# Values of each pair of token blocks projected beside the pair's sums, products on raw weights first, output-weight steps paced

## The chip, the cores and the metric

One core of a Trainium2 chip runs the whole layer. The metric is the device time of one execution in microseconds (us). The engines: TensorE (PE; its weight loads are the row PEld), VectorE (DVE), ScalarE (ACT), GpSimd (POOL) and SyncE (SP), which issues DMAs here and computes nothing. ACT issues DMAs too.

## What is computed

One mixer layer over 2048 latent tokens (a 32 x 64 grid) and 256 context tokens, width 1024: normalisation and modulation give h; one projection of h into eight groups of 512 columns; neighbourhood attention on one half of the groups, retention on the other; gates; one output projection with its own gate; a residual and a last normalisation.

```python
p = h @ w_in      # h: (2304, 1024), w_in: (1024, 4096)
# columns: NA q 0 | NA k 512 | NA v 1024 | NA gate 1536 | RET q 2048 | RET k 2560 | RET v 3072 | RET gate 3584
y = concat(neighbourhood_attention(q, k, v, k_ctx, v_ctx) * silu(gate), retention(rq, rk, rv) * silu(rgate))
out = rmsnorm(x + ada_gate * (y @ w_out))
```

Everything is float32. Each operand is split into a high part, rounded to fp32r, and a low part, the rest; a product is three matmuls: high x high, low x high, high x low.

## The kernel before

The latent tokens are four blocks of 512, the context is block 4. The parts of h of a block are two tiles of SBUF, high and low, of 2 MB each. Blocks 0 and 1 lie in the pool `hx`, 2 and 3 in `hy`, and there is no room for more: from some point on, blocks lie in DRAM (`hS`) and are reloaded. Weights of 256 columns come as two raw tiles `st` (four in all, so two sets of columns) and are split into `whi` and `wlo` by `w_split` (ACT casts, POOL or DVE subtracts); there are two pairs.

The program is one list of instructions per engine, in the order in which the Python code emits them, and a DMA stands on its issuing engine's queue in that order. A `unit` is one projection of 256 columns: `u_k` (K), `u_v` (values of attention, 256 tokens), `u_rk`, `u_rv`, `u_rq` (retention). One is 48 matmuls of 256 columns for values, in eight yields. `tick()` issues the stores deferred by earlier units, and `hooks` are functions called between pieces.

The order of the work around the change:

- K windows (`window(b)`, L485, b = 0 to 4): 32 steps each, in which the blocks' h is also prepared; window 4 is the context's and half as long.
- Values of blocks 2 and 3, 8 units, two spill steps (a DMA of 0.5 MB into `hS`) after each, so 16 in all; then 2 units of context values; then 8 units of blocks 0 and 1, beside which `h_sums(T, 0, 1)` (L514) makes four sums of half blocks in the tiles of `hy`. It is ten functions: VectorE and POOL add and subtract, ACT rounds the high part (L524), DVE or POOL make the low part (L525).
- `strassen(T, 0, 1, ...)`: six sets of 256 columns (`SETS`: NA gate, RET gate, NA q). A set (`w_set`, L609) computes a 2 x 2 block product for the two token blocks by seven products of half size instead of eight. Four products use a sum of weights, made by `w_sums` (L569) in four parts p0 to p3 from the raw weights; POOL makes the low parts (L580), ACT the high (L579). Parts of the next set's sums are called at four steps in the set: p0 after the second product, then p1, p2 and p3. Blocks 0 and 1 are spilled meanwhile, one DMA a step.
- Reload of blocks 2 and 3 into `hx`, and four units of the context for retention (`u_rk`, `u_rv`). Then 4 units `u_rv` of 256 columns at 3072 for blocks 2 and 3, beside `h_sums(T, 2, 3)`.
- `strassen(T, 2, 3, ...)`, with `wo_steps`: `wo_open`, eight `wo_gate` (each adds a row block of w_ada into the gate row `gacc`, L688), `wo_row` (two matmuls that spread the row, L695), eight `wo_mul` m0 to m7 (a row block of w_out times the gate row, L699, split and stored). The row block is one tile, `wraw`, loaded by SP (L685) after each step. One step of the list is called per step of a set.
- 24 fill steps (`LEAD`): a fill step is one yield of the units of a stream of retention projections; attention calls the rest of the stream between the parts of its 128 tiles, and the retention comes behind. `NF` counts 44 units of 8 steps.

Line numbers are those of the kernel before. In `w_set` the products are issued in this order, with `W` the weights' sums, `t` the tokens' sums and `b` raw blocks:

```python
nc.scalar.copy(yb, prod(W["a11"], b11))
V(xa, prod(W["a12"], b21), yb, ALU.add)
step(0)
m4 = prod(W["a22"], t4)
...
V(xb, prod(W["s2"], t2), yb, ALU.add)
step(1)
m5 = prod(W["s1"], t1)
V(yb, prod(W["s3"], t3), xb, ALU.add)
...
step(2)
m3 = prod(W["s4"], b22)
...
step(3)
```

Of the kernel before, what the change touches and what calls it, by code (L numbers as in the profile page):

```python
# [82 lines left out]
def hybrid_kernel(ctx: ExitStack, tc: tile.TileContext, a: dict, out: bass.AP):  # L83
# [390 lines left out]
    fseq = [(u_rv, 3328), (u_rk, 2560), (u_rq, 2048), (u_rk, 2816), (u_rq, 2304)]  # L474
    fseq += [(u_rv, 3328), (u_rv, 3072), (u_rk, 2560), (u_rq, 2048)]
    MID = [(2560, u_rk), (2816, u_rk), (3328, u_rv), (3072, u_rv)]
    wseq = [1280, *SETS, *[c0 for c0, _ in MID], *SETS, fseq[0][1], fseq[1][1]]
    wcur = []

    def load_w():  # L480
        if wseq:
# [1065 lines left out]
```

## Time and profile before

| | us |
|---|---|
| median of 3 runs | 1485.26 (1485.07 to 1489.99) |
| the profiled execution | 1483.65 |
| its span in the trace | 1481.8 |
| TensorE busy in the span | 1335.8 (90%) |
| VectorE, ScalarE, POOL busy | 787.6, 590.4, 628.7 |
| mean granted clock of TensorE | 0.962 of full |

The span is what the trace covers; the time of the execution has about 2 us around it. A row of the timeline is: start in us, duration of the stretch in us, engine, line of the kernel, operation, output tile <- input tiles, shape, count in the stretch, and in brackets how long the engine had been idle and what released it.

### The profile page before, as it was taken

The page shows a single profiled execution, that of the slowest core. Times are in us where ns is not written, and L with a number is a line of the kernel's source. Part 1 is how long each engine was busy: PE and PEld are TensorE (multiplying, and loading weights), DVE is VectorE, ACT ScalarE, POOL GpSimd, SP SyncE. Part 2 cuts the span into 40 slices and gives each one's busy share as a digit, 9 for nine tenths or more (in the row PEclk, how much of TensorE's full clock was granted, in tenths as well). Part 3 has the DMA queues.
Part 4 walks back from the last instruction along what each step waited for, and adds up shares of the span by engine and source line. Part 5 has one row for each costly group of instructions (what it writes and reads, how often), then busy time and mean ns, then how long its engine had stood idle before and what let it go on. Part 6 is the DMA issues. An engine that isn't in the chain of part 4 may idle for free.

```text
span 1481.8 us, 23106 instructions
## 1 busy us (share of the span) xinstructions
PE 1335.8 (90%) x8236; PEld 1165.8 (79%) x8236; DVE 787.6 (53%) x1420; ACT 590.4 (40%) x1245; POOL 628.7 (42%) x585
## 2 busy tenths in 40 slices
PE   6989999489989397766999999999999989999997
PEld 2467999478878285546998999999999879888886
DVE  5786116333424463342678777777665554444435
ACT  4544212233231233322655655555665233334332
POOL 4442312354444454542454643445453234544442
PEclk9999999699999598888999999999999999999999
DMA  9544692366483056656886779995754998655533
GB/s 307 163 157 142 226 303 94 116 221 229 163 310 130 29 171 199 221 205 191 202 230 198 210 221 266 265 250 163 209 159 127 293 283 260 227 174 168 170 122 121
DMA packets 228596, 292.49 MB, mean 197 GB/s; under 512 B 17537, under 2 KB 169217, under 8 KB 227458
## 3 DMA queue, kind: packets, MB, share of 16 engines
q1 hardware_dynamic: 192674, 227.30, 51.4%
q10 hardware_dynamic: 35808, 63.72, 12.2%
q8 instruction: 66, 1.08, 0.3%
q14 instruction: 48, 0.39, 0.1%
HBM read 193.43 MB, written 97.52 MB: 196 GB/s over the span
## 4 chain that ended last, share of the span: by engine, by line
PE 42%; issue 4%; DVE 4%; DMA 4%; POOL 3%; ACT 2%; SPq 1%; ACTq 0%; POOLq 0%; DVEq 0%
PE mm L1391 10%; PE mm L365 8%; PE sS L952 5%; PE mm L354 4%; PE tr L979 3%; PE po L1000 3%; PE mm L1114 2%; PE tr L981 2%; PE po L1002 2%; DMA v<-rvS 1%; PE mm L1303 1%; PE mm L1302 1%; PE mm L1301 1%; POOL g L704 1%; PE mm L1282 1%
## 5 line engine op out<-in xcount | busy, mean ns | idle before, releaser
L365 PE MATMUL mm<-whi,hhi 128*128 128x256 f32 x768 | 225.4, 293 | 7.8 <-DVE o L406 7.8
L365 PE MATMUL mm<-wlo,hhi 128*128 128x256 f32 x768 | 218.6, 285 | 3.6 <-POOL wlo L338 3.6
L365 PE MATMUL mm<-whi,hlo 128*128 128x256 f32 x768 | 217.8, 284 | 0.0
L983 ACT CAST pt<-tr 128x640 fp32r<-128x640 f32 (+1 forms) x128 | 95.7, 748 | 153.9 <-PE tr L981 152.5
L365 PEld LDWEIGHTS mm<-whi,hhi 128*128 128x128 f32 x768 | 147.5, 192 | 8.0 <-issue 8.0
L972 POOL TENSOR_SCALAR sp<-sp,stt 128x640 f32<-128x640 f32 (+2 forms) x128 | 103.5, 812 | 116.8 <-DVE stt L971 100.2
L365 PEld LDWEIGHTS mm<-wlo,hhi 128*128 128x128 f32 x768 | 146.9, 191 | 4.5 <-POOL wlo L338 4.5
L365 PEld LDWEIGHTS mm<-whi,hlo 128*128 128x128 f32 x768 | 147.8, 192 | 0.0
L989 DVE TENSOR_TENSOR pt<-tr,pt 128x640 fp32r<-128x640 f32 (+1 forms) x128 | 113.9, 890 | 63.6 <-ACT pt L983 62.3
L961 DVE CUSTOM_DVE_ANT_0 sp<-sS,nb 128x640 f32<-128x640 f32 (+2 forms) x128 | 105.4, 824 | 31.1 <-DMA nb<-in_rpb_t_dram 24.0
L966 ACT ACTIVATE sp<-sp,stt 128x640 f32<-128x640 f32 (+2 forms) x128 | 107.4, 839 | 29.8 <-DVE stt L961 28.7
L622 PE MATMUL mm<-hhi,whi 128*128 128x512 f32 x336 | 101.4, 407 | 17.9 <-ACT whi L579 15.1
L338 POOL TENSOR_TENSOR wlo<-st,whi 128x256 fp32r<-128x256 f32 (+1 forms) x75 | 86.2, 1165 | 68.3 <-ACT whi L336 62.4
L952 PE MATMUL sS<-k,q 128*128 128x256 f32 (+3 forms) x512 | 100.4, 318 | 14.0 <-DMA q<-qS 10.6
L354 PE MATMUL mm<-hhi,whi 128*128 128x512 f32 x256 | 107.3, 419 | 0.0
L354 PE MATMUL mm<-hlo,whi 128*128 128x512 f32 x256 | 101.0, 394 | 5.5 <-DVE hlo L271 2.3
L354 PE MATMUL mm<-hhi,wlo 128*128 128x512 f32 x256 | 101.2, 395 | 0.0
L952 PEld LDWEIGHTS sS<-k,q 128*128 128x128 f32 x512 | 82.7, 189 | 21.0 <-issue 10.7
L1391 PE MATMUL mm<-wor,y 128*128 128x512 f32 x384 | 95.4, 397 | 1.2 <-DVE xt L1400 1.2
L580 POOL TENSOR_TENSOR whi<-st,whi 128x512 fp32r<-128x512 f32 x48 | 63.3, 1340 | 76.6 <-ACT whi L579 75.1
L622 PEld LDWEIGHTS mm<-hhi,whi 128*128 128x128 f32 x336 | 65.7, 196 | 35.0 <-ACT whi L579 15.7
L622 PE MATMUL mm<-hhi,wlo 128*128 128x512 f32 x240 | 73.9, 424 | 18.3 <-ACT o L651 10.7
(252 smaller groups left out, 3059.8 us busy)
## 6 DMA issues: line engine op xcount, KB each, us to landing
st<-in_w_in_dram SPq DMA_DIRECT2D x58, 512.0 KB
q<-qS SPq DMA_DIRECT2D x64, 256.0 KB
k<-kS SPq DMA_DIRECT2D x16, 576.0 KB
kS<-o SPq DMA_DIRECT2D x16, 512.0 KB
hS<-hhi SPq DMA_DIRECT2D x16, 512.0 KB
hS<-hlo SPq DMA_DIRECT2D x16, 512.0 KB
qS<-o ACTq DMA_DIRECT2D x16, 512.0 KB
hhi<-hS SPq DMA_DIRECT2D x16, 512.0 KB
```

The source lines that it names most:

```text
L338: eng.tensor_tensor(l, r, f(h), ALU.subtract)
L354: nc.tensor.matmul(pm[:, :n], ww[:, k, cs], h[:, k, :], start=(k == 0 and i == 0), stop=(k == KC - 1 and i == 2))
L365: nc.tensor.matmul(pm[:, t * WG:(t + 1) * WG], h[:, k, o:o + P], ww[:, k, :], start=(k == 0 and i == 0), stop=(k == KC - 1 and i == 2))
L580: nc.gpsimd.tensor_tensor(t[:, 1], r, f(t)[:, 0], ALU.subtract)
L622: nc.tensor.matmul(pm, ww[:, k, :], hh[:, k, :], start=(k == 0 and i == 0), stop=(k == KH - 1 and i == 2))
L952: nc.tensor.matmul(o, hd["q"][i][:, hl, j * P:(j + 1) * P], k, start=(hl == 0), stop=(hl == 1))
L961: nc.vector.tensor_tensor_reduce(T["sp"][:, :n], T["s"], nbz[big][:, o:o + n], -1.0, 3e38, ALU.add, ALU.min, T["st"][:, 0:1])
L966: nc.scalar.activation(sp[:, :n], sp[:, :n], AF.Exp, bias=st[:, 0:1], scale=-1.0, accum_out=st[:, 1:2])
L972: nc.gpsimd.tensor_scalar(sp[:, :n], sp[:, :n], st[:, 2:3], 0.0, ALU.mult, ALU.add)
L983: nc.scalar.copy(pt[:, :ng_ + 2, 0, :], tr[:, :ng_ + 2, :])
L989: nc.vector.tensor_tensor(pt[:, :n, 1, :], tr[:, :n, :], f(pt)[:, :n, 0, :], ALU.subtract)
L1391: nc.tensor.matmul(pm, yy[:, k, :], ww[:, k, sl], start=(k == 0 and i == 0), stop=(k == 3 and i == 2))
```

## The change

1. The spill of blocks 2 and 3 moves from the value units into the K windows 3 and 4: one DMA at every fourth step.
2. The values of blocks 2 and 3 are no longer projected ahead of the first sets. They are projected after the reload, beside `h_sums(T, 2, 3)`, as those of blocks 0 and 1 are beside `h_sums(T, 0, 1)`. A new function `values` does both. The weights at 1024 and 1280 are loaded and split a second time for that. Every fifth yield calls one of the ten functions of the sums, the first sum of the weights (p0) is made after the fifth unit, the others after the loop.
3. The four units `u_rv` at 3072 that stood there go into the attention fill; `NF` is 48 units, `LEAD` 32 steps. Blocks 3 and 2 change places in the order of the fill and of the reload.
4. In a set the order of products is a11, a12, s4, a22, s2, s3, s1. Of the weights' sums p1 and p2 are called together at the third step, and p3 holds two cuts and the next load. The split of the weights that follow the last set moves to the third step too.
5. In `h_sums`, `fourth` is all on VectorE, in a tile used in halves, and the low part of key 4 goes to POOL.
6. In `wo_steps` a step without work stands after g1, g3, g5 and g7, and another ahead of the row.

```diff
-LEAD = 24
+LEAD = 32
...
-    fseq = [(u_rv, 3328), (u_rk, 2560), (u_rq, 2048), (u_rk, 2816), (u_rq, 2304)]
+    fseq = [(u_rv, 3072), (u_rk, 2560), (u_rq, 2048), (u_rv, 3328), (u_rk, 2816), (u_rq, 2304)]
...
-    wseq = [1280, *SETS, *[c0 for c0, _ in MID], *SETS, fseq[0][1], fseq[1][1]]
+    wseq = [1280, *SETS, 2560, 2816, 3328, 3072, 1024, 1280, *SETS, fseq[0][1], fseq[1][1]]
...
             run_acts(32 * b + n)
+            if b > 2 and n % 4 == 3:
+                spill_step()
...
-            (G if key < 3 else V)(t[:, 1, ks, :], d, f(t)[:, 0, ks, :], ALU.subtract)
+            (V if key == 3 else G)(t[:, 1, ks, :], d, f(t)[:, 0, ks, :], ALU.subtract)
...
-            o = env["st"].tile([P, 2, 512], F32, name="o3", bufs=1)
-            d, e = o[:, 0, :], o[:, 1, :]
+                tl["o"] = env["st"].tile([P, 2, 512], F32, name="o3", bufs=1)
+            d = tl["o"][:, k % 2, :]
             V(d, bh[:, k, :], ah[:, k, :], ALU.subtract)
-            G(e, bl[:, k, :], al[:, k, :], ALU.subtract)
-            V(d, d, e, ALU.add)
+            V(d, d, bl[:, k, :], ALU.add)
+            V(d, d, al[:, k, :], ALU.subtract)
...
         def p2():
+            cut("s4", 3, 0, a12)
+
+        def p3():
+            cut("s3", 2, 1, a21)
             cut("s1", 2, 0, a22)
-            cut("s3", 2, 1, a21)
-
-        def p3():
-            cut("s4", 3, 0, a12)
             load_w()
 
-        return W, [p0, p1, p2, p3]
+        return W, [p0, None, lambda: (p1(), p2()), p3]
...
-        return [None, p1, None, load_w]
+        return [None, None, p1, None]
...
         step(0)
+        m3 = prod(W["s4"], b22)
+        fin(oa, 0, A)
         m4 = prod(W["a22"], t4)
-        fin(oa, 0, A)
+        step(1)
         V(xb, prod(W["s2"], t2), yb, ALU.add)
-        step(1)
-        m5 = prod(W["s1"], t1)
         V(yb, prod(W["s3"], t3), xb, ALU.add)
         oc, (_, xc) = out_tile()
         V(xc, m4, yb, ALU.add)
+        V(xb, m3, xb, ALU.add)
+        fin(oc, 1, A)
+        step(2)
+        m5 = prod(W["s1"], t1)
         od, (_, xd) = out_tile()
...
+    def values(ws, bb, hs, W):
+        ahead = [None] * 4
+        vu = [(w, c0, tp) for w, c0 in zip(ws, (1024, 1280)) for b in bb for tp in (2 * b, 2 * b + 1)]
+        y = 0
+        for n, (w, c0, tp) in enumerate(vu):
+            for _ in u_v(w, c0, tp):
+                y += 1
+                if hs and y % 5 == 0:
+                    hs.pop(0)()
+            tick()
+            if n == 4:
+                W, ahead = w_sums(wcur.pop(0))
+                ahead[0]()
+        while hs:
+            hs.pop(0)()
+        ahead[2]()
+        ahead[3]()
+        return W
...
-    wo_steps = [wo_open, None] + [g(k) for k in range(8)] + [wo_row] + [m(k) for k in range(8)]
+    seq = [wo_open] + [g(k) for k in range(8)] + [None, wo_row] + [m(k) for k in range(8)]
+    wo_steps = []
+    for n, e in enumerate(seq):
+        wo_steps += [e, None] if n in (2, 4, 6, 8) else [e]
```

Three places, as the engines' instruction lists have them. SP's queue at the end of the K windows, before (`kS` are the stores of K, `st` weights, `vB` values, `hS_0_91` and `hS_1_92` block 2's parts in DRAM, 93 and 94 block 3's):

```order
L150 DMA kS_64<-o 256x1x512
L150 DMA kS_61<-o 256x1x512
L176 DMA st<-in_w_in_dram 128x4x256 x4
L150 DMA kS_62<-o 256x1x512
L150 DMA kS_63<-o 256x1x512
L150 DMA kS_64<-o 256x1x512
L150 DMA kS_61<-o 256x1x256
L150 DMA kS_62<-o 256x1x256
L150 DMA kS_63<-o 256x1x256
L150 DMA kS_64<-o 256x1x256
L176 DMA st<-in_w_in_dram 128x4x256 x4
L506 DMA hS_0_91<-hhi 128x1024 x2
```

and after:

```order
L150 DMA kS_64<-o 256x1x512
L488 DMA hS_0_91<-hhi 128x1024 x2
L150 DMA kS_61<-o 256x1x512
L176 DMA st<-in_w_in_dram 128x4x256 x4
L488 DMA hS_0_91<-hhi 128x1024 x2
L150 DMA kS_62<-o 256x1x512
L488 DMA hS_1_92<-hlo 128x1024 x2
L150 DMA kS_63<-o 256x1x512
L488 DMA hS_1_92<-hlo 128x1024 x2
L150 DMA kS_64<-o 256x1x512
L488 DMA hS_0_93<-hhi 128x1024 x2
L150 DMA kS_61<-o 256x1x256
```

The spill of block 2 stood behind the last K stores and weight loads; it now stands among the stores, and the first `st` loads are between its parts.

ScalarE in the third set of the first six (COPY of the first product, CASTs of the weights' sums, ACTIVATEs and stores of the gate's output tiles), before:

```order
L651 COPY o3_2604<-mm_2605 128x512
L579 CAST whi_2633<-st_2454 128x512
L579 CAST whi_2633<-st_2456 128x512
L636 ACTIVATE o_2603<-o_2603 128x512
L150 DMA gS2_71<-o_2603 128x512
L579 CAST wlo_2668<-st_2456 128x512
L579 CAST wlo_2668<-st_2454 128x512
L636 ACTIVATE o_2705<-o_2705 128x512
L150 DMA gS3_72<-o_2705 128x512
L579 CAST whi_2712<-st_2456 128x512
L579 CAST whi_2712<-st_2454 128x512
```

and after:

```order
L652 COPY o3_2105<-mm_2106 128x512
L580 CAST whi_2134<-st_1955 128x512
L580 CAST whi_2134<-st_1957 128x512
L637 ACTIVATE o_2104<-o_2104 128x512
L150 DMA gS2_71<-o_2104 128x512
L637 ACTIVATE o_2197<-o_2197 128x512
L150 DMA gS3_72<-o_2197 128x512
L580 CAST wlo_2202<-st_1957 128x512
L580 CAST wlo_2202<-st_1955 128x512
L580 CAST wlo_2211<-st_1957 128x512
L637 ACTIVATE o_2228<-o_2228 128x512
L637 ACTIVATE o3_2105<-o3_2105 128x512
```

The cuts `wlo` of the next set's sums stood ahead of the second output tile's ACTIVATE; they now stand behind it and its store.

VectorE around the values (L406 is the low part of a value tile, the others are the sums), before:

```order
L406 TENSOR_TENSOR o<-mm,o 128x4x64 x22
L533 TENSOR_TENSOR hhi<-hhi 128x1024
L535 TENSOR_TENSOR hhi<-hhi 128x1024
L525 TENSOR_TENSOR hlo<-hhi,hlo 128x1024
L533 TENSOR_TENSOR hhi<-hhi 128x1024
L535 TENSOR_TENSOR hhi<-hhi 128x1024
L525 TENSOR_TENSOR hlo<-hhi,hlo 128x1024
L543 TENSOR_TENSOR hhi<-hhi 128x1024
L544 TENSOR_TENSOR hhi<-hhi,hlo 128x1024
```

and after, with the lines of the sums one number further down in the code:

```order
L406 TENSOR_TENSOR o<-mm,o 128x4x64 x4
L534 TENSOR_TENSOR hhi<-hhi 128x1024
L536 TENSOR_TENSOR hhi<-hhi 128x1024
L526 TENSOR_TENSOR hlo<-hhi,hlo 128x1024
L406 TENSOR_TENSOR o<-mm,o 128x4x64 x2
L534 TENSOR_TENSOR hhi<-hhi 128x1024
L536 TENSOR_TENSOR hhi<-hhi 128x1024
L526 TENSOR_TENSOR hlo<-hhi,hlo 128x1024
L544 TENSOR_TENSOR hhi<-hhi 128x1024
L545 TENSOR_TENSOR hhi<-hhi,hlo 128x1024
```

Eleven units' value passes stood in a row ahead of the first sum; now two passes or four stand ahead of each sum.

## Rows read from the trace of the kernel before

**Rows 1.** The page, the span in 40 slices: TensorE's busy tenths and granted clock.
```profile
PE   6989999489989397766999999999999989999997
PEclk9999999699999598888999999999999999999999
```

**Rows 2.** Windows by stage: us, busy us by engine (instructions), granted clock, DMA share, GB/s.
```profile
163.20:291.20 128.00, 106.49 (x866) 105.71 (x864) 42.31 (x56) 22.92 (x46) 31.26 (x16) 0.93 0.59 187
291.20:416.50 125.30, 121.38 (x505) 97.27 (x506) 49.67 (x77) 43.54 (x77) 58.35 (x44) 0.97 0.58 198
416.50:473.40 56.90, 50.01 (x386) 49.19 (x385) 15.76 (x14) 13.30 (x17) 22.32 (x11) 0.94 0.72 268
473.40:579.80 106.40, 68.92 (x262) 52.78 (x261) 55.41 (x63) 31.73 (x53) 53.41 (x35) 0.81 0.34 109
579.80:699.50 119.70, 84.99 (x395) 69.16 (x393) 38.04 (x47) 34.12 (x55) 52.61 (x40) 0.87 0.65 207
699.50:1143.00 443.50, 436.29 (x3252) 412.87 (x3252) 324.17 (x725) 252.95 (x522) 209.46 (x232) 1.00 0.75 208
```

**Rows 3.** Windows without a wait, lines L365 and L622: us, TensorE, its weight loads.
```profile
180.00:220.00 40.00, 40.00 (x336) 40.00 (x335) 1.00 0.94 302
...
340.00:400.00 60.00, 60.00 (x261) 48.73 (x261) 1.00 0.55 193
```

**Rows 4.** Timeline, TensorE: matmuls behind the waits that end the stages.
```profile
291.21 0.79 PE L622 MATMUL mm<-hhi,whi 128*128 128x512 f32 x1 [11.90 <-ACT whi L579]
...
498.50 5.99 PE L622 MATMUL mm<-hlo,wlo 128*128 128x512 f32 x12 [19.49 <-ACT wlo L579]
...
624.95 0.79 PE L622 MATMUL mm<-hhi,wlo 128*128 128x512 f32 x1 [7.81 <-ACT o L651]
...
699.49 1.25 PE L952 MATMUL sS<-k,q 128*128 128x288 f32 x4 [10.55 <-DMA q<-qS]
```

**Rows 5.** Timeline, VectorE and POOL beside the values: passes of the sums.
```profile
246.70 5.86 POOL L525 TENSOR_TENSOR hhi<-hhi 128x1024 fp32r<-128x1024 f32 x2 [53.19 <-ACT hhi L524]
...
250.22 3.41 DVE L552 TENSOR_TENSOR hhi<-hhi 128x1024 f32<-128x1024 f32 x1 [2.30 <-POOL hhi L525]
...
258.13 1.22 DVE L552 TENSOR_TENSOR hhi<-hhi 128x1024 f32<-128x1024 f32 x1
...
270.78 0.42 DVE L406 TENSOR_TENSOR o<-mm,o 128x256 fp32r<-128x256 f32 x1 [0.44 <-ACT o L405]
```

**Rows 6.** Timeline, end of the last K window: ScalarE's copy, POOL's weight split.
```profile
160.90 0.37 ACT L374 CAST o<-mm 128x256 fp32r<-128x256 f32 x1 [3.07 <-DMA kS<-o]
...
162.30 2.37 POOL L338 TENSOR_TENSOR wlo<-st,whi 128x1024 fp32r<-128x1024 f32 x1 [11.94 <-ACT whi L336]
```

**Rows 7.** Timeline of a set, the next set's sums: cuts, low parts, last sum.
```profile
350.00 0.62 ACT L579 CAST wlo<-st 128x512 fp32r<-128x512 f32 x1 [3.59 <-PE mm L622]
350.70 1.29 POOL L580 TENSOR_TENSOR wlo<-st,wlo 128x512 fp32r<-128x512 f32 x1 [2.72 <-ACT wlo L579]
...
354.20 0.69 DVE L591 TENSOR_TENSOR st<-st 128x512 f32<-128x512 f32 x1
...
354.90 1.30 POOL L580 TENSOR_TENSOR wlo<-st,wlo 128x512 fp32r<-128x512 f32 x1 [2.91 <-ACT wlo L579]
```

**Rows 8.** Tile wraw: ns min/median/max, first and last start; then waiters (us, times).
```profile
L688 DVE SCALAR_TENSOR_TENSOR gacc<-wraw,silc,gacc x8: 1277/1476/2218, 529.2 to 571.3; 128x1024 f32<-128x1024 f32 x8
...
L699 DVE TENSOR_TENSOR wraw<-wraw,gacc x8: 1215/1225/1226, 579.8 to 652.8; 128x1024 f32<-128x1024 f32 x8
...
  PE mm L695: 10.2, 1
```

**Rows 9.** Timeline after the first sets: reload, weight load, cast of those weights.
```profile
417.92 0.46 SPq L758 DMA_DIRECT2D hhi<-hS  x1
...
430.32 0.38 SPq L176 DMA_DIRECT2D st<-in_w_in_dram  x1
...
439.82 1.04 ACT L336 CAST whi<-st 128x1024 fp32r<-128x1024 f32 x1 [6.12 <-DMA st<-in_w_in_dram]
```

More of the change, by code (lines that the diff above doesn't have):

```diff
@@ L482, in load_w, with spill_step @@
             wcur.append(w_raw(wseq.pop(0)))
+    spill = [(b, hl, k) for b in (2, 3, 0, 1) for hl in range(2) for k in range(0, KC, 2)]
+    def spill_step():
+        if spill:
+            b, hl, k = spill.pop(0)
+            nc.sync.dma_start(hS[b][hl][:, k * 512:(k + 2) * 512], f(blk[b][hl])[:, k:k + 2, :].rearrange("p k t -> p (k t)"))
     def window(b):
@@ L737, in hybrid_kernel @@
     T = []
-    hs = h_sums(T, 0, 1)
-    W, ahead = w_sums(wcur.pop(0))
-    for n, (w, c0, tp) in enumerate([(w, c0, tp) for w, c0 in ((w0, 1024), (w1, 1280)) for tp in range(4)]):
-        for _ in u_v(w, c0, tp):
-            if hs and n:
-                hs.pop(0)()
-        tick()
-        if n == 4:
-            ahead[0]()
-        if n == 5:
-            ahead[1]()
-    while hs:
-        hs.pop(0)()
-    ahead[2]()
-    ahead[3]()
+    W = values((w0, w1), (0, 1), h_sums(T, 0, 1), None)
     mid = []
     strassen(T, 0, 1, W, [spill_step] * 24, mid)
-    while spill:
-        spill_step()
+    for d in reload_parts(3):
+        nc.sync.dma_start(*d)
+    (wk0,) = mid
+    load_w()
     for d in reload_parts(2):
         nc.sync.dma_start(*d)
-    (wk0,) = mid
     wk1 = w_split(wcur.pop(0))
     load_w()
-    for d in reload_parts(3):
-        nc.sync.dma_start(*d)
     unit(u_rk(wk0, 2560, 8))
     wk2 = w_split(wcur.pop(0))
+    load_w()
     unit(u_rk(wk1, 2816, 8))
@@ L768, in hybrid_kernel @@
     load_w()
+    unit(u_rv(wk2, 3328, 8))
+    w0 = w_split(wcur.pop(0))
     load_w()
-    unit(u_rv(wk2, 3328, 8))
     unit(u_rv(wk3, 3072, 8))
+    w1 = w_split(wcur.pop(0))
+    load_w()
     T = []
-    hs = h_sums(T, 2, 3)
-    W, ahead = w_sums(wcur.pop(0))
-    ahead[0]()
-    for n in range(4):
-        for _ in u_rv(wk3, 3072, 4 + n):
-            if hs:
-                hs.pop(0)()
-        tick()
-        if n == 0:
-            ahead[1]()
-    while hs:
-        hs.pop(0)()
-    ahead[2]()
-    ahead[3]()
-    wo_steps = [wo_open, None] + [g(k) for k in range(8)] + [wo_row] + [m(k) for k in range(8)]
+    W = values((w0, w1), (3, 2), h_sums(T, 2, 3), None)
+    g = lambda k: lambda: wo_gate(k)
+    m = lambda k: lambda: wo_mul(k)
+    seq = [wo_open] + [g(k) for k in range(8)] + [None, wo_row] + [m(k) for k in range(8)]
+    wo_steps = []
+    for n, e in enumerate(seq):
+        wo_steps += [e, None] if n in (2, 4, 6, 8) else [e]
     last = []
@@ L840, in next_c @@
             return w
-        order = [(kind, *a_) for kind, c0 in fseq[:3] for b in (2, 3) for a_ in units(kind, b)]
-        order += [(kind, *a_) for b in (2, 3, 0, 1) for kind, c0 in fseq[3:5] for a_ in units(kind, b)]
-        order += [(kind, *a_) for kind, c0 in fseq[5:] for b in (0, 1) for a_ in units(kind, b)]
+        order = [(kind, *a_) for kind, c0 in fseq[:4] for b in (3, 2) for a_ in units(kind, b)]
+        order += [(kind, *a_) for b in (3, 2, 0, 1) for kind, c0 in fseq[4:6] for a_ in units(kind, b)]
+        order += [(kind, *a_) for kind, c0 in fseq[6:] for b in (0, 1) for a_ in units(kind, b)]
         at = [0]
@@ L868, in steps @@
                 yield v
-        for m, (kind, c0) in enumerate(fseq[:3]):
+        for m, (kind, c0) in enumerate(fseq[:4]):
             wn = next_c() if m else w2
-            for n, args in enumerate(units(kind, 2) + units(kind, 3)):
+            for n, args in enumerate(units(kind, 3) + units(kind, 2)):
                 yield from steps(kind(w, c0, *args))
@@ L889, in fill_stream @@
         load_w()
-        for m, (kind, c0) in enumerate(fseq[5:]):
+        for m, (kind, c0) in enumerate(fseq[6:]):
             wn = next_c() if m < 3 else None
```

22 lines of the change are left out of this document (3 added, 19 removed).

## The prediction

> **What bounds the kernel now.** I read the page's slices first [rows 1]. TensorE is busy at nine tenths nearly everywhere; the exceptions are the start, slices 13 to 19 (roughly 450 to 700 us of the span) and the tail. The granted clock is down in slices 14 to 18 too. So the change is worth what its stages lose, and the second view cuts the span into them [rows 2]: A is the values (163.20 to 291.20), B the six sets of blocks 0 and 1, C the context units and the reload, D the sets of blocks 2 and 3 until the first output-weight product m0, E from m0 to attention's first product (699.50), and the last row is attention, where TensorE is busy 436.29 of 443.50 us at full clock. There every microsecond of TensorE work counts whole.
>
> What TensorE needs without a wait comes from two stretches without one [rows 3]. In 40 us of units it did 336 matmuls, 0.119 us each: a unit of 48 is 5.71 us, a fill step of 6 is 0.714. In 60 us of sets it did 261, 0.230 each: a product of 12 is 2.76, a set of seven 19.3. Against that the stages of before stand so. A: 18 units, 102.8 of 128.0. B: 115.9 of 125.3. C: 8 units, 45.7 of 56.9. D: 3 sets and the gate row, 60 of 106.4. E: 3 sets and 24 fill steps, 75.0 of 119.7. About 137 us of 536.3 are lost, 91 of them in D and E. The stage ends are set by the waits of [rows 4]: 11.90 for the first weight cut in B; 19.49 for a cut of the sums in D, after which 12 matmuls took 5.99 us instead of 2.76 while the clock came back; 7.81 for ScalarE behind an m step; 10.55 at the end of E for the last stored q.
>
> **The change part by part.** Work as such is only moved: eight units go from A to C and D's beginning, four units of retention values leave C and D for the attention fill, eight more fill steps run ahead of attention.
>
> *Stage A* becomes 2 context units and 8 units of blocks 0 and 1: 57.1 us. The spill of blocks 2 and 3, once between the moved units, now goes into the last two K windows, on the queue SP, among the stores of K and ahead of the weight loads. Sixteen transfers of 0.52 MB are 8.4 MB; the windows' own stores and loads are some 5.2 MB; at 302 GB/s [rows 3] all of it takes 45 us, and the windows last 96 matmuls of 0.230 and 96 of 0.119, 33.5 us. So their stores can be up to 11.5 us late, or not at all if the queue keeps up. What waits for them is plain: ScalarE's copy of the last K unit already waited 3.07 us for a store's buffer, and the casts and the splits on POOL that make the next weights stand behind it [rows 6]. I take the middle, 6 us, then 2 for the clock and 1 for the second split: 9, between 0 and the 25.2 that A loses now. A: 66.1.
>
> The sums beside eight units of 45.7 us need VectorE for 14 passes of 1.22 us, 12 of 0.69 and 16 of 0.42, 32.1 us [rows 5, 7], and POOL for 6 passes of 2.37 and 6 of 1.30, 22.0 us [rows 6, 7]. Either one fits alone. I cost this at nothing; the cover is the 45.7 us, and what it costs if that fails is a rival.
>
> *Stage B.* The products that use raw weights now come first (a11, a12, then s4, a22, s2, s3, s1) and the cut of a22 with the sums moves from the second step to the third. The chain from there is in [rows 7]: cut at 350.00, its low half at 350.70, four sums, cut of s2 and its low half from 354.90 to 356.20: 6.2 us, and s4's low half is one POOL pass more, 7.5. The cut now stands in ScalarE's order behind the work on the output tile, which waits for the s3 product; I put its start 2.5 us after that product. Then come s1 (2.76) and the next a11 and a12 (5.52), and the third matmul of the next s4, 0.46 in, needs the low half: 8.7 us of room against 10.0, so 1.3, say 1.4 with the granularity of a pass. Bounds: nothing (no set of before waited at this place) and 5 us, where the ScalarE work ahead of the cut takes two output tiles and their stores instead of one. I take 1.4, as its parts all have rows. The first set has no set before it; its sums start when the values end: between 1.4 and the 11.90 now seen there I take 7.5. B: 115.9 + 7.5 + 5 x 1.4 = 130.4, five more than now. The raw-first order itself takes the 11.90 wait away from B's start, but that wait lies in A's row.
>
> *Stage C* is 4 context units and 8 units of values, 68.5 us. Its weights are the question. The split of the first one moves one step later, two products: up to 5.5, I take 5. The reload began at 417.92, a weight load stood behind its first eight transfers at 430.32 and was cast from 439.82 after 6.12 us of waiting [rows 9]. The fourth context unit's weights (3072) now stand behind all sixteen: 12.4 us later, so issued at about 442.7 and split at about 455, where the unit could start at 416.5 + 5 + 17.1 = 438.6. That is up to 16; since the queue may have drained, 10, with 5 as the low end. 5 more for the clock after such a wait (the 5.99 of [rows 4] is 3.2 above normal, and I allow for more than one). C: 88.5; between 79.5 and 95.
>
> *Stage D* is now 4 sets, since m0 comes at the end of the fourth: 77.2, 2 for the row, 7.5 for the first set's sums as in B, and 3 x 1.4. The 19.49 wait goes, because values stand beside the sums; the gate row's own wait of 10.2 goes, because a step without work stands ahead of it. The gate steps were 6.0 us apart [rows 8]; eight of them in twelve steps and some 60 us have room. D: 90.9; at least 79.2, and with that 10.2 still there 101.
>
> *Stage E.* The eight m steps are a chain of their own: load, multiply, cut, store, with one buffer for the row. They ran from 579.8 to 652.8, 10.4 us apart [rows 8], whatever TensorE had to do. Nothing in the change shortens a link, so it stays 73.0. But it now runs in sets 5 and 6, and one set of 19.3 that came after it is gone: 46.7 - 19.3 = 27.4 from the last m to attention, and the eight more fill steps (5.7) lie in the 10.55 wait for q. With 1.6 for ends that do not fit: E = 102.0; from 83 (the chain hidden in part, since steps are paced) to 119.7 as now.
>
> *Attention* gets 24 steps more to fill (four units, 32 steps, less the 8 ahead of it): 24 x 0.714 = 17.1, whole, as TensorE is the bound there.
>
> **The sum.** 66.1 + 130.4 + 88.5 + 90.9 + 102.0 = 477.9 against 536.3: 58.4 earlier; less 17.1: 41.3. The profiled execution took 1483.65 us (its span 1481.8), the median of the runs is 1485.26, so the profile stands for the median to 0.1%. 1485.3 - 41.3 = 1444.
>
> [...] In A, VectorE's sum took 3.41 us where the same form elsewhere took 1.22; POOL was in two passes of 5.86 us at that time [rows 5]. [...]
>
> **The rivals.** (1) *The forecast*, 1425 to 1460, 0.62. (2) *All of it is covered*: the spill keeps up, the s4 sums are in time, the last weights arrive. Then 9 + 14.5 + 20 + 11.7 of the terms shrink to about a third, some 35 us less: 1399 to 1420. For it speaks that B lost only 9.4 us in six sets; against it that the room of 8.7 us is under the chain's 10.0. 0.14. (3) *VectorE and POOL in turns* beside eight units: 32.1 + 22.0 = 54.1 against 45.7, 8.4 a stage, twice 16.8: 1461. For it the 3.41 [rows 5]; against it that stage A has room for 42.31 and 31.26 one after the other in 128.0 and showed the wait once. 0.12. (4) *The change does not do what it says*: the transfers only change place, the K stores and then the context units wait as long as the values did. Stage A keeps 25.2 of waits, C takes all of its 26: 16 + 6 back, and the sets of D wait for reloads by another 12: about 1478. 0.07. (5) *Slower*: the cut of a22 waits behind the output tiles' activations and store issues on ScalarE in each set. When it is 3.6 us later than I put it, each set waits 5 us, and if TensorE's clock falls as after the 19.49 gap, another 3.2: (5 - 1.4 + 3.2) x 12 = 82, to 1526. Without the clock it decides from 41.3 / 12 = 3.4 us a set on. For it: ScalarE is the releaser of the waits in [rows 4]; against it: its rows in [rows 7] are 0.62 us each, and it is busy 43.54 of 125.30 in B [rows 2]. 0.05.
>
> **How the numbers follow.** Predicted: 1444. The range 1416 to 1472 leaves out half of (2), most of (4) and (5): 0.18. A measurement here tells half a per cent, 7.4 us, from no change. Faster by more: (1), (2), (3) and 0.03 of (4): 0.91. Within: 0.04. Slower: (5), 0.05.
>
> **What would show it.** In the profile after: the wait ahead of A's first unit on ScalarE's copy or the split (6 us) and K stores waiting on the spill; in each set one wait of TensorE in the s4 product, released by POOL, near 1.4 us; TensorE waiting for the fourth context unit's weights; no gap near 19 us before the third stage's sets; m steps still 10.4 us apart; attention longer by 17. Wrong it would be if the s4 wait is over 3 us with a lower granted clock in every set, if VectorE's sums are near 3 us throughout, or if the m steps come closer together than 10 us or spread beyond 11.

## The result and the profile after

The changed kernel took 1492.56 us (median of 14 runs, 1488.23 to 1497.21) against 1485.09 for the kernel before in the same comparison: a ratio of 1.005, interval 1.0034 to 1.0067. So it is half a per cent slower, where 41 us less were forecast. (Two medians further down count in one run that is far longer than the rest, 5818 and 2476 us; this moves them by 0.2 us at most, and the ratios leave it out.) The profiled execution has a span of 1489.9 us, 8.1 longer than before.

The page of the kernel after, TensorE's busy tenths and its granted clock, answers to [rows 1]:

```profile
PE   6999896999795889648999999999999989999997
PEclk9999997999797899779999999999999999999999
```

The weak stretch is still there, from slice 11 to 19 where it was 14 to 19. By stage, as in [rows 2] (us, busy us of TensorE, weight loads, VectorE, ScalarE, POOL, then granted clock, DMA share, GB/s; A to E and attention):

```profile
163.20:230.30 67.10, 60.46 (x487) 59.78 (x486) 35.87 (x41) 19.14 (x33) 27.57 (x13) 0.95 0.62 208
230.30:374.50 144.20, 123.36 (x507) 95.75 (x505) 53.58 (x79) 43.28 (x78) 55.88 (x44) 0.94 0.53 183
374.50:466.20 91.70, 75.44 (x577) 74.32 (x577) 39.69 (x37) 25.98 (x37) 46.05 (x21) 0.88 0.63 216
466.20:581.00 114.80, 96.42 (x362) 73.99 (x363) 49.60 (x67) 33.03 (x61) 48.78 (x35) 0.87 0.43 138
581.00:685.30 104.30, 65.20 (x340) 55.03 (x339) 32.33 (x35) 28.72 (x47) 48.21 (x36) 0.81 0.66 221
685.30:1133.00 447.70, 438.49 (x3278) 415.33 (x3279) 320.93 (x717) 251.57 (x525) 210.12 (x236) 1.00 0.77 208
```

| stage | forecast | measured | miss |
|---|---|---|---|
| A, values of blocks 0 and 1 | 66.1 | 67.1 | 1.0 |
| B, six sets | 130.4 | 144.2 | 13.8 |
| C, context and values of blocks 2 and 3 | 88.5 | 91.7 | 3.2 |
| D, four sets to m0 | 90.9 | 114.8 | 23.9 |
| E, m steps to attention | 102.0 | 104.3 | 2.3 |
| attention to the end, against before | +17.1 | +22.3 | 5.2 |

Attention starts at 685.30 instead of 699.49, 14 us earlier and not 58. B and D, the two stages of sets, hold 38 of the 49 us that are missing. TensorE's waits in them and at the starts of A and of the fill steps, from the timeline of the kernel after (start, duration, line, in brackets the idle time before and its releaser; compare [rows 4]):

```profile
168.88 0.58 PE L365 MATMUL mm<-whi,chi 128*128 128x256 f32 x1 [5.01 <-ACT whi L336]
...
248.56 0.79 PE L623 MATMUL mm<-hhi,wlo 128*128 128x512 f32 x1 [12.45 <-ACT wlo L580]
...
274.19 0.73 PE L623 MATMUL mm<-hhi,wlo 128*128 128x512 f32 x2 [1.07 <-POOL wlo L581]
...
466.17 0.80 PE L623 MATMUL mm<-hhi,whi 128*128 128x512 f32 x1 [7.53 <-ACT whi L580]
...
485.27 0.79 PE L623 MATMUL mm<-hhi,wlo 128*128 128x512 f32 x1 [10.70 <-ACT wlo L580]
...
511.54 0.73 PE L623 MATMUL mm<-hhi,wlo 128*128 128x512 f32 x2 [2.11 <-POOL wlo L581]
...
652.66 0.58 PE L365 MATMUL mm<-whi,hhi 128*128 128x256 f32 x1 [19.23 <-ACT whi L336]
```

The big waits of before have moved, not gone: 11.90 before the first product of B is now 12.45 before its third, 19.49 in D is now 7.53 and 10.70. All are waits for ScalarE's cuts of the weights: 7.53 for the raw a11 ahead of D's first product, 12.45 and 10.70 for the sum s4 ahead of the third. And there is a new one in nearly every set: about 1.1 us in B, 2.1 in D. Counting 84 matmuls to a set, the sets of B follow each other in 19.45 us before the change. After it they follow in 21.0 to 21.1 in B, and in 23.9, 24.1 and 25.4 in D (the last of these with the two matmuls of the gate row). The first set takes 36.4 in B and 36.7 in D.

The last wait of the list, 19.23 us, stands behind the sets, ahead of the first fill step. The split of its weights now comes a step later, and ScalarE, behind an m step and an output tile that waits for VectorE, reaches it at 651.56:

```profile
651.56 1.99 ACT L336 CAST whi<-st 128x1024 fp32r<-128x1024 f32 x2 [1.84 <-DVE o L633]
```

The row of the m steps answers to [rows 8]:

```profile
L700 DVE TENSOR_TENSOR wraw<-wraw,gacc x8: 1216/1226/1927, 581.0 to 654.7; 128x1024 f32<-128x1024 f32 x8
```

They take 73.7 us where 73.0 were forecast.

### The profile page after: what moved, and what is told of

The parts are those of the page before. It is cut to its first block, busy times and chain, and to the rows that moved or that the text cites. A ratio compares the mean times of both kernels' runs of the same rounds, so it can differ in the third digit from the quotient of the medians.

```text
span 1489.9 us, 23084 instructions
## 1 busy us (share of the span) xinstructions
PE 1343.9 (90%) x8236; PEld 1169.6 (79%) x8236; DVE 797.9 (54%) x1424; ACT 594.5 (40%) x1257; POOL 639.9 (43%) x593
## 4 chain that ended last, share of the span: by engine, by line
PE 44%; DMA 5%; DVE 4%; issue 3%; POOL 2%; ACT 2%; ACTq 0%; SPq 0%; DVEq 0%; POOLq 0%
PE mm L365 10%; PE mm L1386 10%; PE sS L947 4%; PE mm L354 4%; PE tr L974 3%; PE po L995 3%; PE mm L1109 2%; PE tr L976 2%; PE po L997 2%; DMA v<-rvS 1%; PE mm L1298 1%; PE mm L1297 1%; PE mm L1296 1%; PE mm L1277 1%; DMA rvS<-o 1%
## 5 line engine op out<-in xcount | busy, mean ns | idle before, releaser
L365 PE MATMUL mm<-whi,hhi 128*128 128x256 f32 x768 | 225.7, 294 | 19.2 <-ACT whi L336 19.2
L365 PE MATMUL mm<-wlo,hhi 128*128 128x256 f32 x768 | 218.4, 284 | 2.0 <-POOL wlo L338 2.0
L365 PE MATMUL mm<-whi,hlo 128*128 128x256 f32 x768 | 217.9, 284 | 0.0
L365 PEld LDWEIGHTS mm<-whi,hhi 128*128 128x128 f32 x768 | 147.7, 192 | 19.7 <-ACT whi L336 19.7
L365 PEld LDWEIGHTS mm<-wlo,hhi 128*128 128x128 f32 x768 | 147.2, 192 | 2.6 <-POOL wlo L338 2.6
L365 PEld LDWEIGHTS mm<-whi,hlo 128*128 128x128 f32 x768 | 147.9, 193 | 0.0
L338 POOL TENSOR_TENSOR wlo<-st,whi 128x256 fp32r<-128x256 f32 (+1 forms) x87 | 102.9, 1197 | 87.1 <-ACT whi L336 74.6
L623 PE MATMUL mm<-hhi,wlo 128*128 128x512 f32 x240 | 78.4, 443 | 43.1 <-ACT wlo L580 28.4
L581 POOL TENSOR_TENSOR wlo<-st,wlo 128x512 fp32r<-128x512 f32 x36 | 49.7, 1396 | 137.1 <-ACT wlo L580 137.1
L354 PE MATMUL mm<-hhi,wlo 128*128 128x512 f32 x256 | 101.7, 397 | 0.3 <-DVE wlo L338 0.3
L623 PEld LDWEIGHTS mm<-hhi,wlo 128*128 128x128 f32 x240 | 49.1, 209 | 64.2 <-ACT wlo L580 33.2
L947 PEld LDWEIGHTS sS<-k,q 128*128 128x128 f32 x512 | 83.3, 189 | 17.2 <-DVE stt L956 8.1
```

The costliest lines, as they stand in the source:

```text
L338: eng.tensor_tensor(l, r, f(h), ALU.subtract)
L354: nc.tensor.matmul(pm[:, :n], ww[:, k, cs], h[:, k, :], start=(k == 0 and i == 0), stop=(k == KC - 1 and i == 2))
L365: nc.tensor.matmul(pm[:, t * WG:(t + 1) * WG], h[:, k, o:o + P], ww[:, k, :], start=(k == 0 and i == 0), stop=(k == KC - 1 and i == 2))
L581: nc.gpsimd.tensor_tensor(t[:, 1], r, f(t)[:, 0], ALU.subtract)
L623: nc.tensor.matmul(pm, ww[:, k, :], hh[:, k, :], start=(k == 0 and i == 0), stop=(k == KH - 1 and i == 2))
L947: nc.tensor.matmul(o, hd["q"][i][:, hl, j * P:(j + 1) * P], k, start=(hl == 0), stop=(hl == 1))
```

## What the experiments showed

The theory was that the new order in the sets eats the gain: s4 is the last of the sums to be made and now the third to be used, so each set waits for the chain that makes it. Rivals were the DMA traffic, ScalarE's lag behind TensorE at the end of the value units, and VectorE and POOL in each other's way.

### The order of before put back

```diff
-        m3 = prod(W["s4"], b22)
         m4 = prod(W["a22"], t4)
+        fin(oa, 0, A)
         V(xb, prod(W["s2"], t2), yb, ALU.add)
+        step(1)
+        m5 = prod(W["s1"], t1)
...
+        step(2)
+        m3 = prod(W["s4"], b22)
...
-        return W, [p0, None, lambda: (p1(), p2()), p3]
+        return W, [p0, p1, p2, p3]
...
-        return [None, None, p1, None]
+        return [None, p1, None, None]
```

> The changed kernel with the products and the four parts of the weights' sums in the order and at the steps of the kernel before. Theory (the new order itself costs 1.57 us in each set of blocks 0 and 1 and 4.4 in each of 2 and 3): these sets are 19.45 apart again, 21 us less, and the first sets wait for a22 about as long as they now wait for s4: about 1472. Rival (the loss is that of the stages, not of the order): sets stay at 21 to 24, 1488 to 1496.

Measured: 1452.17 us, ratio to the kernel before 0.9784 (0.9761 to 0.9806). It is 40 us less than the changed kernel, twice what was expected. Its windows of B and D (columns as above):

```profile
231.70:358.70 127.00, 119.31 (x507) 95.81 (x506) 51.52 (x77) 43.67 (x78) 60.32 (x46) 0.97 0.62 213
...
449.70:547.20 97.50, 90.73 (x368) 71.16 (x369) 50.08 (x67) 33.26 (x62) 49.52 (x36) 0.94 0.51 162
```

and TensorE's waits in the two first sets, now for the cut of a22:

```profile
245.05 0.80 PE L623 MATMUL mm<-hlo,wlo 128*128 128x512 f32 x1 [7.57 <-ACT wlo L580]
...
463.84 0.79 PE L623 MATMUL mm<-hlo,wlo 128*128 128x512 f32 x1 [6.04 <-ACT wlo L580]
```

B is 17.2 us shorter, D 17.3, E 3.9; C is nearly the same (91.0). In B the sets follow in 19.45 us again. The first waits fall too, by 4.9 and 4.7, and the first sets take 29.7 and 30.6 us: that half was not in the expectation. The likely reason is that a cut is ready before a sum.

### The new order alone, on the kernel before

The same edit the other way round, and nothing else of the change. It is not the exact reverse in the first sets: the kernel before makes their cut of a22 and the sums while value units still run, this one behind them, and the run above leaves them behind.

> The kernel before, with only the new order of the products and the new steps of the weights' sums. Theory (the order costs by itself): sets of blocks 0 and 1 are 21.0 apart instead of 19.45, those of 2 and 3 near 24, the first sets wait 5 us more; 5 x 1.6 + 3 x 4.4 + 10 = 31 us more, about 1516. Rival (the order only costs together with the values moved into the second stage): within 7 us of 1486.

Measured: 1528.20 against 1487.76, ratio 1.0272 (1.0256 to 1.0288): 40.4 us more. So the order's price is about 40 us with or without the other parts, and the other parts together are worth 33. Its windows of the two stages of sets:

```profile
294.80:436.90 142.10, 124.85 (x505) 96.67 (x505) 51.90 (x78) 43.08 (x77) 53.64 (x42) 0.95 0.51 176
496.00:617.10 121.10, 73.18 (x274) 55.26 (x273) 54.49 (x62) 30.23 (x51) 51.68 (x34) 0.79 0.29 96
```

and, from its timeline, the first s4 of D, where only four units lie beside the sums of the tokens:

```profile
535.88 0.79 PE L622 MATMUL mm<-hhi,wlo 128*128 128x512 f32 x1 [34.23 <-ACT wlo L579]
```

### The chain started earlier, in the new order

```diff
         V(xb, prod(W["s2"], t2), yb, ALU.add)
+        if ahead[4]:
+            ahead[4]()
...
-        return W, [p0, None, lambda: (p1(), p2()), p3]
+        return W, [p0, None, None, p3, lambda: (p1(), p2())]
```

> The changed kernel, but in each set the cut of a22, the sums and the cuts of s2 and s4 stand right behind the s2 product instead of behind s3 and the output tile's ACTIVATE. Theory (the s4 product waits for the next set's sums, and where the clock falls in that wait the set pays again): the wait of 1.07 in each set of blocks 0 and 1 and of 2.1 in each of blocks 2 and 3 goes, and the falls at 512, 536 and 560 us with it; sets are 19.45 us apart as in the kernel before instead of 21.0 and 23.9. 5 x 1.57 + 3 x 4.4 = 21 us less than the 1492.6 of the changed kernel: about 1472. Rival (the sets are slow for the order of products or for the DMA traffic beside them): the sets keep their 21.0 and 23.9, time within 5 us of 1492.

Measured: 1463.58, ratio 0.9848 (0.9826 to 0.9871), 29 us less than the changed kernel. Sets of B and D are 19.45 apart, but for one of 21.1 that holds the gate row. The first waits stay (12.46 and 10.67). The order of the products is still the new one, so the waits inside the sets are those of the chain, and neither the order by itself nor the traffic beside the sets. The rest of the 40 us, 11, is about what the first sets take more than in the old order (35.7 and 36.7 us against 29.7 and 30.6). The chain itself, in the kernel after, second set (ScalarE's cut of a22, POOL's low part, VectorE's last sum, the cut of s4, POOL's last two low parts, TensorE):

```profile
266.72 0.62 ACT L580 CAST wlo<-st 128x512 fp32r<-128x512 f32 x1 [0.48 <-ACT o L637]
...
267.42 1.29 POOL L581 TENSOR_TENSOR wlo<-st,wlo 128x512 fp32r<-128x512 f32 x1 [12.09 <-ACT wlo L580]
...
270.92 0.69 DVE L592 TENSOR_TENSOR st<-st 128x512 f32<-128x512 f32 x1
...
271.70 0.62 ACT L580 CAST wlo<-st 128x512 fp32r<-128x512 f32 x1 [0.16 <-DVE st L592]
...
271.62 2.51 POOL L581 TENSOR_TENSOR wlo<-st,wlo 128x512 fp32r<-128x512 f32 x2 [2.91 <-ACT wlo L580]
```

It starts 2.66 us after the s3 product (which ends at 264.06) and takes 7.4 to POOL's end at 274.13; TensorE goes on at 274.19.

### Why a set of D pays three times as much

In the timeline of D the same two POOL passes take 3.55 us. They stand beside a pass of the gate row on VectorE:

```profile
507.84 1.28 DVE L689 SCALAR_TENSOR_TENSOR gacc<-wraw,silc,gacc 128x1024 f32<-128x1024 f32 x1
...
507.93 3.55 POOL L581 TENSOR_TENSOR wlo<-st,wlo 128x512 fp32r<-128x512 f32 x2 [2.91 <-ACT wlo L580]
```

Windows around the wait of 1.07 in the second set of B and around the last set's in B, then before, behind and after the wait of 2.11 (columns as above; the granted clock is the third number from the end):

```profile
272.00:276.00 4.00, 2.87 (x12) 1.81 (x11) 0.81 (x2) 2.62 (x5) 3.50 (x4) 1.00 0.39 135
...
357.00:363.00 6.00, 4.67 (x19) 3.54 (x20) 3.06 (x4) 2.51 (x5) 3.69 (x4) 1.00 0.44 174
...
490.00:512.00 22.00, 19.69 (x81) 15.36 (x80) 9.03 (x12) 4.28 (x8) 6.87 (x5) 0.96 0.48 151
512.00:515.50 3.50, 3.50 (x11) 2.67 (x10) 0.45 (x1) 1.64 (x5) 2.50 (x2) 0.53 0.64 202
515.50:536.00 20.50, 18.03 (x77) 14.03 (x76) 11.52 (x14) 5.88 (x11) 8.77 (x6) 1.00 0.45 149
```

The experiment shortens the gate pass:

```diff
-        nc.vector.scalar_tensor_tensor(wo["acc"], wo["w"], silc[:, k, 0:1], wo["acc"], ALU.mult, ALU.add)
+        nc.vector.scalar_tensor_tensor(wo["acc"][:, 0:16], wo["w"][:, 0:16], silc[:, k, 0:1], wo["acc"][:, 0:16], ALU.mult, ALU.add)
```

> The changed kernel, with the eight gate-row accumulations on VectorE done on 16 columns of 1024 only (the rest of the row is left out; loads, steps and all else stay). Theory (a set of blocks 2 and 3 waits 2.1 us for the s4 sums, not 1.07, because a gate pass of 1.3 to 2.2 us stands on VectorE ahead of the sums, and that longer gap is what the clock falls after): these sets go from 23.9 apart to 21.1, as in blocks 0 and 1, without a fall of the clock: 8 us less, about 1484. Rival (their wait comes from traffic or from POOL, not from the gate): they stay at 23.9 and the time within 3 us of 1492.

Measured: 1485.81, ratio 0.9995 (0.9976 to 1.0014), 7 us less than the changed kernel. The set behind the first of D is 21.2 us long instead of 23.9. Two matmuls of its s4 product, at 513.81 behind the wait, took 0.62 us, as behind the wait of 1.07 in B at a clock of 1.00; at 512.43 in the kernel after, behind the wait of 2.11 and at a clock of 0.53, two took 1.05:

```profile
510.34 0.23 DVE L689 SCALAR_TENSOR_TENSOR gacc<-wraw,silc,gacc 128x16 f32<-128x16 f32 x1
...
510.43 2.53 POOL L581 TENSOR_TENSOR wlo<-st,wlo 128x512 fp32r<-128x512 f32 x2 [2.91 <-ACT wlo L580]
...
513.01 0.73 PE L623 MATMUL mm<-hhi,wlo 128*128 128x512 f32 x2 [1.09 <-POOL wlo L581]
```

The gate pass is the cause in this set, but not as the expectation put it: it stands behind the sums on VectorE, not ahead of them. Beside it POOL took 3.55 us for the two passes, beside the short one 2.53, so 1.02 more; that makes the wait 2.11 instead of 1.09; and behind that longer wait the clock is at 0.53 for 3.5 us, which costs another 1.7 us. The third of these sets, with the gate row, took 22.8 instead of 25.4.

The second still took 23.4, with waits of 0.71 and 1.07 in the s4 product and the clock at 0.51 behind them:

```profile
523.89 0.24 DVE L689 SCALAR_TENSOR_TENSOR gacc<-wraw,silc,gacc 128x16 f32<-128x16 f32 x1 [5.30 <-DMA wraw<-in_w_ada_dram]
...
527.37 0.62 ACT L580 CAST wlo<-st 128x512 fp32r<-128x512 f32 x1 [0.45 <-ACT o L637]
...
535.60:539.00 3.40, 3.40 (x9) 2.61 (x8) 0.69 (x1) 2.19 (x5) 3.09 (x3) 0.51 0.39 89
```

There the gate pass stood on VectorE until its row block had landed, the output tile's additions stood behind it, and the cut of a22 came 3.4 us after the s3 product instead of 2.7. This is read from the trace; no run tested it. The last set of B has nearly the same pair of waits, 0.66 and 1.07, and kept the clock at 1.00 (the second window above). So the length of a wait alone does not tell here whether the clock falls.

### What sets the first waits

At the end of A TensorE is through with the eight units at 230.29. VectorE ends the last sum of the tokens at 235.05; ScalarE begins to copy the last unit at 239.56, issues its stores and cuts a22 only at 242.99:

```profile
234.36 0.69 DVE L565 TENSOR_TENSOR o<-o,hlo 128x512 f32<-128x512 f32 x1
...
239.56 0.37 ACT L405 CAST o<-mm 128x256 fp32r<-128x256 f32 x1 [2.72 <-DMA vB<-o]
...
241.28 1.67 ACTq L415 DMA_DIRECT2D vB<-o  x4
242.99 0.62 ACT L580 CAST wlo<-st 128x512 fp32r<-128x512 f32 x1 [2.20 <-DMA vB<-o]
```

Four runs tried causes of this lag of some 12.7 us. In the changed kernel, the cut of a22 and the sums called after the sixth unit (`if n == 5: ahead[4]()`):

> The changed kernel, but the first set's cut of a22, the sums and the cut of s2 are called after the sixth of the eight value units instead of after the last. Theory (the first s4 product waits because its chain of sums starts only when ScalarE is through with all value units, 9 us behind TensorE): only one cut of s4 is left for the end, the first waits of 12.45 and 10.70 become 8 to 9 and 6 to 7, and about 8 us are won, 1484. Rival (ScalarE is late as a whole, so what is put earlier delays the copies of the last units by as much): waits within 1.5 us of 12.45 and 10.70, time within 4 us of 1492.

Measured: 1494.29, ratio 1.0067 (1.0045 to 1.0089). The theory fails: the first waits become longer, 14.54 and 12.59, by more even than the rival allowed, and the time stays. What was put ahead in ScalarE's queue delayed the rest of it here.

All value stores on SP (`enumerate((nc.sync, nc.sync))`):

> The changed kernel, but all stores of values are issued on SP, none on ScalarE. Theory (ScalarE's lag behind TensorE at the end of the values comes from its four DMA issues a unit, 2.04 us each time): ScalarE has 16 us less in each of the two value stages, its last copy follows the last unit by under 4 us instead of 9.3, the first s4 waits fall to 5 to 7 us and the 7.53 ahead of the second stage's first product goes: 15 to 20 us less, about 1475. Rival (VectorE and POOL taking turns over the sums, or the landing of the stores, sets the lag): the waits stay within 2 us and so does the lag, 1488 to 1496; with SP issuing twice as many it may grow.

Measured: 1487.05, ratio 1.0002 (0.9984 to 1.0021), 5.5 us less, a third of what the theory wanted: the waits are 10.19, 4.86 and 11.28. ScalarE cuts a22 10.3 us behind the last unit instead of 12.7, so its issues are a part of the lag and not its main part.

The order of before in the sets, and all low parts of the token sums on VectorE (`V(t[:, 1, ks, :], ...)`):

> The kernel with the order of before in the sets (1452), and the low parts of the token sums all on VectorE, none on POOL. Theory (ScalarE's lag at the end of the values comes from VectorE and POOL taking turns: passes of 2.06, 3.46 and 1.67 where 1.22 and 0.69 are normal): VectorE has 7.7 us more work and no long passes, the lag of 9 us falls to 5, the waits of 7.57, 7.53 and 6.04 fall by 3 to 4 each: 8 to 10 us less, about 1443. Rival (the lag is the to and fro of ScalarE and VectorE over value copies and sums in their fixed order): within 4 us of 1452, or slower by the 7.7 twice.

Measured: 1457.93, ratio 0.9815 (0.9792 to 0.9838), 6 us more than with POOL; waits of 7.44, 8.70 and 6.31. The long passes of VectorE beside POOL are there in the kernel after (3.46 us at 449.13, with POOL in a pass of 2.40 from 449.12; 1.22 on the same line at 446.73), but to take POOL away costs more than they do.

Each cut of a token sum put one call later, so that ScalarE does not stand at the head of its queue waiting for VectorE:

```diff
+        def late(*x):
+            cuts.append(x)
+
+        def go(fn, c):
+            if cuts:
+                cut(*cuts.pop(0))
+            if fn:
+                fn(c)
...
-            cut(3, ks, d)
+            late(3, ks, d)
```

> The kernel of 1446 (old order, m step that frees its row early, value stores on SP); ScalarE's cut of each token sum is put one call later, ahead of the next sum on VectorE. Theory (ScalarE is 9 us behind TensorE at the end of the values because each cut, at the head of its queue, waits 2.4 to 3.7 us for VectorE's sum while copies of finished units stand behind it): those waits go, the last copy follows the last unit by under 4 us, and the waits of 3.7, 4.9 and 6.6 before and in the first sets shrink to 2 or less each, with the clock's falls: 10 to 14 us less, about 1434. Rival (the time of VectorE's passes beside POOL's sets the lag): within 4 us of 1446.

Measured: 1438.46, ratio 0.9683 (0.9660 to 0.9705), against 1445.85 without it. The wait ahead of D's first product falls from 4.87 to 1.33 and the other first waits stay (3.69 for 3.73, 6.28 for 6.55). So this to and fro is a part of the lag in the second value stage. In the first it is not: ScalarE cuts a22 8.6 us after the last unit, at 239.69, where it was 8.7 without the edit. In that trace VectorE ends the last sum of the tokens 4.5 us behind TensorE, two units' copies stand behind it on ScalarE, and one of these waits 1.20 us for a store's buffer; what would shorten this was not tried.

```profile
234.88 0.69 DVE L574 TENSOR_TENSOR o<-o,hlo 128x512 f32<-128x512 f32 x1
...
238.56 0.37 ACT L405 CAST o<-mm 128x256 fp32r<-128x256 f32 x1 [1.20 <-DMA vB<-o]
...
239.69 0.62 ACT L589 CAST wlo<-st 128x512 fp32r<-128x512 f32 x1
...
240.37 0.79 PE L632 MATMUL mm<-hlo,wlo 128*128 128x512 f32 x1 [3.69 <-ACT wlo L589]
```

### The chain of the m steps

On the kernel with the old order, VectorE writes the product into the staging tile, where it is split in place:

```diff
-        nc.vector.tensor_tensor(wo["w"], wo["w"], wo["acc"], ALU.mult)
...
-            nc.scalar.copy(w[:, 0, :], wo["w"][:, sl])
-            nc.gpsimd.tensor_tensor(w[:, 1, :], wo["w"][:, sl], f(w)[:, 0, :], ALU.subtract)
+            nc.vector.tensor_tensor(f(w)[:, 1, :], wo["w"][:, sl], wo["acc"][:, sl], ALU.mult)
+            nc.scalar.copy(w[:, 0, :], f(w)[:, 1, :])
+            nc.gpsimd.tensor_tensor(w[:, 1, :], f(w)[:, 1, :], f(w)[:, 0, :], ALU.subtract)
```

> The kernel with the order of before in the sets (1452), and in the m steps VectorE writes the product into the staging tile, where ScalarE and POOL split it, so that the row buffer is free for the next load after VectorE's pass and not after POOL's. Theory (the end of the sets is set by the chain of the m steps, 10.4 us a link, of which about 3.8 are the casts and POOL's passes): links of 6.5 to 8, m0 to m7 in 50 us instead of 72, attention 15 to 20 us earlier, about 1435. Rival (the two staging tiles and their stores bind next, or the sets do): links above 9.5, time within 5 us of 1452.

Measured: 1450.56, ratio 0.9768 (0.9743 to 0.9793), against the 1452.17 of the kernel without the edit, within the spread of the runs. The rival holds: links are 9.9 us, and VectorE now waits for the stores of the staging tiles:

```profile
556.31 0.69 DVE L703 TENSOR_TENSOR g<-wraw,gacc 128x512 f32<-128x512 f32 x1 [6.57 <-DMA woS<-g]
```

With the value stores on SP too:

> As the one before, and all value stores on SP. Theory: with ScalarE's issues gone the first sets' waits (7.57, 7.53 and 6.04 with the old order) shrink as they did in the changed kernel, by some 5 us in all: about 5 us less than the one before. Rival (SP's loads now stand behind the stores): no gain, within 3 us of the one before.

Measured: 1445.85, ratio 0.9734 (0.9706 to 0.9761), 4.7 less, as expected. The two intervals overlap; the traces support the gain, since the first sets' waits add up to 15.2 us instead of 19.4. With the m stores issued on SP at once instead of at ScalarE's next step:

> The kernel of 1446; the four stores of an m step are issued on SP at once, behind the next row's load, not on ScalarE at the next step. Theory (a link of the m chain is now set by the staging tiles' stores, which wait a step for their issue): links of 9.8 us become 7 to 8, m0 to m7 in 53 us instead of 69, attention 10 to 16 us earlier: about 1433. Rival (SP is in order, so the next row's load or the next store waits for POOL's pass on it, or the sets themselves set the pace): links above 9, within 4 us of 1446.

Measured: 1443.97, ratio 0.9708 (0.9692 to 0.9724); m0 to m7 still takes 70.6 us. The rival holds. With both this and the later cuts:

> Both of the last two edits. Theory: their gains add, as they lie in different stages: 20 to 28 us under 1446, about 1422. Rival: where one of them gained nothing, the other's gain alone.

Measured: 1440.26, ratio 0.9678 (0.9653 to 0.9702): the gain of the later cuts alone. What limits a link after these edits stays open.

The fastest of all is the kernel with the old order, the stores on SP, the early release in the m steps and the later cuts: 1438.46 us, 3.2% under the kernel before.

## Why the prediction was wrong

**The parts that held.** The spill in the K windows: A came to 67.1 for 66.1, with 5.01 us of waiting on ScalarE's weight cast where 6 were put, and ScalarE was late there for the K stores, as foreseen:

```profile
167.51 0.37 ACT L374 CAST o<-mm 128x256 fp32r<-128x256 f32 x1 [3.33 <-DMA kS<-o]
```

The m steps: 73.7 for 73.0. C and E were within 3.2 us, but by terms that offset each other, so by luck. In C the fourth context unit waited 5.09 and not 10, and 7.53 stand at its end that were not foreseen. In E the sets ended at 633.4, 21 us ahead of m7, and the wait of 19.23 ahead of the fill steps took this up; neither was foreseen. The whole without the new order took 1452, inside the range that was given; but the forecast had 11 us for that order's waits in the sets, so this does not confirm its sum.

**The step that failed is the cost of the new order.** I had eight sets at 1.4 us for it, 11 in all, and 7.5 for each of the two first sets; to take the order back gained 40. I saw the mechanism and its place: the chain began 2.66 us behind the s3 product and took 7.4, I had put 2.5 and 7.5, and in B each set lost about 1.6 for my 1.4. But I carried these 1.4 into D, three times, where it was 4.4, 4.6 and, with the gate row that I had counted apart as 2, 5.9. The gate pass that lengthens POOL's part was in the diff and in [rows 8], and [rows 5] had VectorE at 3.41 us for 1.22 beside POOL's two passes of 5.86; I used that for the rival on the values only. And I counted a wait as its own length. I had seen the clock lower behind the wait of 19.49, in the row of 5.99 us in [rows 4]. In these sets it was 0.53, 0.52 and 0.51 for 3.5 us behind their waits of 2.11, 2.07 and 2.11, and nearly doubled the cost of each. The sign that I gave for a failure, a wait over 3 us with a lower clock, did not come: here the clock was lower behind waits of 2.07 and 2.11.

**The first sets.** They are the larger part of the miss. I took 7.5 between 1.4 and 11.90. The wait was 12.45 in B and 7.53 with 10.70 in D, and the s4 products behind 12.45 and 10.70 took 6.5 us each. So the first sets of B and D took 17.0 and 17.3 us more than 19.45, which is 9.5 and 9.8 more than I put: 19 of the 38 us that these stages miss. The sets behind the first in D make 9 more. Of the 17 us some 6.5 went with the new order in each stage; the rest stayed with the old one, and the waits in it are for ScalarE. The reason stood in [rows 4]: the waits of 11.90 and 19.49 are for ScalarE's cuts, so ScalarE was behind before. Slice 8 of [rows 1], at four tenths, lies there too, and I left it out of the weak ones. I wrote that the first wait goes from B and that the second goes with the values beside the sums. To move the product to the place behind the waiting one only moves the wait, as long as the same engine is late by as much. The sums beside eight units I cost at nothing, since VectorE and POOL fit into 45.7 us each. By busy time they did (35.87 and 27.57 in A); but the last sum left VectorE 4.8 us behind TensorE's last unit, and ScalarE, whose queue alternates between waiting for VectorE and copying for TensorE, was 12.7 behind though busy for only 19.14.

**The rivals.** The slower case came nearest to what happened: a wait in each set, in D with the clock at 0.51 to 0.53 behind it. I put 5 us of waiting and 3.2 for the clock to it in all twelve, from ScalarE's order; the sets behind the first lost 1.6 in B and about 4.5 in D, and in D it was POOL's passes that made it longer (3.55 us for 2.51). Passes of VectorE that took 3.46 us for 1.22 beside POOL's were seen at the values, yet with the sums' low parts off POOL the kernel was slower (1457.93 for 1452.17, both with the old order).

**What stays open.** Attention and the rest took 5.2 us more than its 144 extra matmuls; about 3.4 of it is a stretch of 6.8 us from 1212 on at a granted clock of 0.50, where the kernel before has 1.00 from 1143 to 1260. One execution of each does not tell more. About 8.6 us of ScalarE's lag at the end of the first value stage, and what sets the pace of the m steps once the row is freed early, stay open too.

## What to carry to other kernels

A reordering that uses a result earlier is priced by the whole chain that makes it, counted from the engine that starts it last, in every stage where it runs and with what else these engines do there. A wait at the head of a stage tells which engine is late; it goes when that engine is made early, not when TensorE is given something else first. And one edit may cost more than all others of a change gain (40 us against 33 here), so each is worth a run alone.

## What the runs showed of the hardware

TensorE's granted clock stayed at 1.00 behind waits of 1.07 to 1.09 us in the sets of B and was 0.53 for 3.5 us behind a wait of 2.11 in D: the twelve matmuls with the wait took 6.93 us there, 4.37 in B, 2.97 without one. The pair of waits of 0.66 and 1.07 in the last set of B left it at 1.00, and one of 0.71 and 1.07 in the kernel with the short gate pass was followed by 0.51.

Two passes of POOL of 2.51 us took 3.55 beside a pass of 1.28 on VectorE, and 2.53 where that pass was 0.23. So POOL took 1.02 us more beside the pass of VectorE that went on for 1.19 us after POOL had begun (507.84 + 1.28, against 507.93).
